# DeltaNet's decay and beta columns computed between tiles of the RG-LRU, on the PSUM tiles of its gates

## The chip, the cores and the metric

The kernel runs on one core of one Trainium2 chip. The metric is the device time of one launch in microseconds (us), as the median of several runs. In the text PE is TensorE (its matmuls), PEld its weight loads, DVE is VectorE, ACT ScalarE, POOL GpSimd and SP SyncE, which here only issues DMAs.

## The reference

One layer of a hybrid decoder on 576 tokens (512 of a prompt and 8 x 8 of samples), model width 1024, in float32. After a norm, one projection `w_in` feeds three branches: an RG-LRU, an S5 state space model and a gated DeltaNet. Their outputs are merged under sigmoid gates, projected and followed by a SwiGLU block. The parts that matter here:

```python
def rglru_branch(xr, gate_in, conv_buf, h0, conv_w, conv_b, wa, ba, wx, bx, lam, w_o):
    xc, new_buf = causal_conv(xr, conv_buf, conv_w)
    xc = xc + conv_b
    xb = xc.reshape(B, T, RG_BLOCKS, RG_BLOCK)
    r = jax.nn.sigmoid(jnp.einsum("btni,nij->btnj", xb, wa).reshape(B, T, RG_WIDTH) + ba)
    i = jax.nn.sigmoid(jnp.einsum("btni,nij->btnj", xb, wx).reshape(B, T, RG_WIDTH) + bx)
    log_a = -RG_C * r * jax.nn.softplus(-lam)
    inp = jnp.sqrt(-jnp.expm1(2.0 * log_a)) * (i * xc)
    h = linear_scan(jnp.exp(log_a), inp, h0)
    return (h * jax.nn.gelu(gate_in)) @ w_o, new_buf, h[:, -1]

# in gdn_branch
    beta = jax.nn.sigmoid(b_in)                                  # (tokens, 4 heads)
    g = -jnp.exp(a_log) * jax.nn.softplus(a_in + dt_bias)        # (tokens, 4 heads)
# in chunk_gated_delta, chunks of 64 tokens
    gc = jnp.cumsum(g, axis=-1)
    decay = jnp.where(causal, jnp.exp(gc[..., :, None] - gc[..., None, :]), 0.0)
```

`beta` and `gc` are the beta and decay columns: 8 numbers for each token, 4 heads of each.

## The kernel before, in words

Activations lie transposed, 128 channels on the partitions and 576 tokens in two halves of 288 columns. A float32 product is made of three fp32r matmuls: the weights are split into a high part `wh` (ACT, L181) and a low part `wl` (DVE, L182), the activations into `hh` and `hl` (for the merge `brh` and `brl`, L236 and L237), and L199, L200 and L201 multiply hh·wh, hl·wh and hh·wl. A raw weight tile `wr` comes by DMA (issued by SP); `wr` has 2 buffers, `wh` and `wl` have 4 each, of 4 k-tiles of 128 rows, so one split feeds 24 matmuls.

PSUM is divided by pools. The projections' and merge's sums `mm` have 3 slots. Tag "sm" has 3 slots: S5's `gtp`, `ktp`, `xp`, `s5yp`, and in the kernel before also `abc`, `gcps` and `bgp`. Tag "sr", which the helper `sr(name)` allocates, has 2 slots and holds the RG-LRU's gate sums `gps` (L748) in this part of the program.

The code is written in this order: S5 in four tiles (`s5_front` and `s5_chain`, L828 to L832); `rg(0)` to `rg(3)`, the RG-LRU's four tiles; five merge gates `g1`; the block of the beta and decay columns (L837 to L905); then the merge of the RG-LRU (`merge("rg_wo", ...)`, tiles 0 to 6, L910), and DeltaNet (`gdn_qkv`, `gdn_prep`). The instructions do not run in the order of the code: a scheduler places each engine's instructions by readiness, priority (the splits of weights stand first) and free slots of the pools, and each engine then runs its list strictly in order. An instruction that waits holds up everything behind it on its engine.

A tile of the RG-LRU, `rg(m)`: two projections, a convolution (L420, DVE), `xc`, four gate matmuls `gps` (L748) each read by a tanh `rgt` on ACT (L749), then exp, tanh and square root (L754 to L758, ACT), products and a scan on DVE (L756 to L769), and the product with the gelu gate (L773). `hout` takes the last states and leaves by `o["rg_h"]` (L907). `tsplit` (L236, L237) splits the result for the merge.

A chain of S5, `s5_chain(m)`: products `z`, the scan `zs` (L674, two for each tile, DVE), `st` (L686), the matmuls `s5yp` (L699, L700), the sum `s5y` (L702, DVE), a gelu (L722 to L726) and eight DMAs `ys` (L707).

The block of the columns: 32 narrow matmuls `abps` (L849), transposes `abc` (L854), a tanh for `beta`, a chain of small softplus instructions on DVE (L120 to L160, then L871, all on 128x20), the cumulative sums `gcps` (L873 to L878, PE), `gc` (L882), exponentials, a transpose `bgp` (L901), its copy `bgs` on ACT (L903), which takes a buffer of S5's scratch (`S5Z`), and a DMA of `bgs` to `bgd` in DRAM (L905). `gdn_prep` reads `bgd` back, spread over the partitions, as `bet` and `eg` (L969), and DVE subtracts `gc` (`dt`, L973).

Of the kernel before, what the change touches and what calls it, by code (L numbers as in the profile page):

```python
# [8 lines left out]
F32 = mybir.dt.float32  # L9
# [56 lines left out]
def hybrid_step(ctx: ExitStack, tc: tile.TileContext, i, o, dbg=None):  # L66
# [13 lines left out]
    def nm(s):  # L80
        cnt[0] += 1
        return f"{s}_{cnt[0]}"
# [9 lines left out]
    def P(k):  # L92
        a, w = PAR[k]
        return par[:, a:a + w]
# [132 lines left out]
    def each(ps, f):  # L227
        for a in range(2):
            f(ps[a], lambda t: t[:, NH * a:NH * a + NH])
# [13 lines left out]
    def tsplit(x, scale=None):  # L243
        return split(x, T("brh", F32R)[:, :NT], T("brl", F32R)[:, :NT], scale)
# [25 lines left out]
    def T(name, dt=F32):  # L270
        return tp.tile([128, TW], dt, name=nm(name), tag="T")

    def sr(name):
        return pss.tile([128, 512], F32, name=nm(name), tag="sr", bufs=2)
# [22 lines left out]
    pss = psx.enter_context(tc.tile_pool(name="pss", bufs=3, space=PSUM))  # L297
# [8 lines left out]
    def R(name):  # L306
        return rp.tile([128, NT], F32, name=nm(name), tag="R")
# [90 lines left out]
    def w_in(idx):  # L398
        return gemm(i["w_in"][idx], h)
# [4 lines left out]
    def pad_in(ps, hist, slot):  # L404
        pad = T("pad")
        smp = pad[:, SOFF:PADW].rearrange("p (b t) -> p b t", t=3 + NTS)
        S.activation(pad[:, 3:3 + NH], ps[0], AF.Copy)  # L407
        S.activation(pad[:, 3 + NH:SOFF], ps[1][:, 0:NP - NH], AF.Copy)
        S.activation(smp[:, :, 3:], ps[1][:, NP - NH:NH].rearrange("p (b t) -> p b t", t=NTS), AF.Copy)
        G.memset(pad[:, 0:3], 0.0)  # L410
        G.tensor_copy(smp[:, :, 0:3], hist.rearrange("p (b t) -> p b t", t=3))
        G.tensor_copy(cst[:, slot, 0, :], pad[:, NP:NP + 3])
        G.tensor_copy(cst[:, slot, 1:9, :], smp[:, :, NTS:])
        return pad

    def conv(pad, w, b):
        y = T("cv")
        S.activation(y[:, :CW], pad[:, 0:CW], AF.Identity, scale=w[0], bias=b)
        for k in range(1, 4):
            V.scalar_tensor_tensor(y[:, :CW], pad[:, k:k + CW], w[k], y[:, :CW], op0=OP.mult, op1=OP.add)  # L420
        return y

    def two_part(t):
        return t[:, 0:NP], t[:, SOFF:SOFF + 11 * NB].rearrange("p (b t) -> p b t", t=11)[:, :, 0:NTS]
# [296 lines left out]
    def gelu2(t, x, sq):  # L721
        S.activation(sq, x, AF.Square)  # L722
        S.activation(sq, sq, AF.Copy, scale=0.044715, bias=1.0)
        V.tensor_tensor(sq, sq, x, op=OP.mult)
        S.activation(sq, sq, AF.Tanh, scale=math.sqrt(2.0 / math.pi))
        V.scalar_tensor_tensor(t, sq, 1.0, x, op0=OP.add, op1=OP.mult)  # L726

    def rg(m):
        ps = w_in(IDX["rgx"] + m)
        pad = pad_in(ps, P("rg_hist")[:, 24 * m:24 * m + 24], m)  # L730
        ps = w_in(IDX["rgg"] + m)
        gx_ = T("rgx")
        each(ps, lambda p, c: S.activation(c(gx_), p, AF.Copy))
        w = P("rg_cw")[:, 4 * m:4 * m + 4]
        y = conv(pad, [w[:, a:a + 1] for a in range(4)], P("rg_cb")[:, m:m + 1])
        xc = R("xc")
        yp_, ys_ = two_part(y)
        S.activation(xc[:, 0:NP], yp_, AF.Copy)
        S.activation(xc[:, NP:NT].rearrange("p (b t) -> p b t", t=NTS), ys_, AF.Copy)
        gts = []  # L740
        rgw = cp.tile([128, 2, 128], F32, name=nm("rgw"), tag="rgw", bufs=2)
        DQ.dma_start(rgw, i["rg_w"][:, 2 * m:2 * m + 2, :])
        for a in range(2):
            t = R("rgt")
            for half in range(2):
                hs = slice(NH * half, NH * half + NH)
                gps = sr("gps")
                PE.matmul(gps[:, 0:NH], rgw[:, a, :], xc[:, hs], start=True, stop=True)  # L748
                S.activation(t[:, hs], gps[:, 0:NH], AF.Tanh, scale=0.5, bias=rc[:, 2 + a, m:m + 1])  # L749
            gts.append(t[:, :NT])  # L750
        tr, ti = gts
        a_ = y[:, :NT]
        th = tr
        S.activation(a_, tr, AF.Exp, scale=rc[:, 1, m:m + 1], bias=rc[:, 1, m:m + 1])  # L754
        S.activation(th, tr, AF.Tanh, scale=rc[:, 0, m:m + 1], bias=rc[:, 0, m:m + 1])
        V.scalar_tensor_tensor(a_, a_, 1.0, th, op0=OP.add, op1=OP.mult)  # L756
        S.activation(a_, a_, AF.Copy, scale=-1.0, bias=1.0)
        S.activation(th, th, AF.Sqrt)  # L758
        V.scalar_tensor_tensor(ti, ti, 1.0, xc[:, :NT], op0=OP.add, op1=OP.mult)
        V.scalar_tensor_tensor(th, a_, 1.0, th, op0=OP.add, op1=OP.mult)  # L760
        V.scalar_tensor_tensor(ti, ti, 0.5, th, op0=OP.mult, op1=OP.mult)
        t8 = cp.tile([128, 8], F32, name=nm("t8"), tag="t8")
        av = a_[:, NP:NT].rearrange("p (b t) -> p b t", t=NTS)[:, :, 0]
        bv = ti[:, NP:NT].rearrange("p (b t) -> p b t", t=NTS)[:, :, 0]
        V.tensor_tensor(t8, av, P("rg_h0")[:, 8 * m:8 * m + 8], op=OP.mult)
        V.tensor_tensor(bv, bv, t8, op=OP.add)
        V.memset(av, 0.0)
        hh = y
        V.tensor_tensor_scan(hh[:, :NT], a_, ti, 0.0, op0=OP.mult, op1=OP.add)  # L769
        G.tensor_copy(hout[:, m, 0:1], hh[:, NP - 1:NP])  # L770
        G.tensor_copy(hout[:, m, 1:9], hh[:, NP:NT].rearrange("p (b t) -> p b t", t=NTS)[:, :, NTS - 1])
        gelu2(gx_[:, :NT], gx_[:, :NT], pad[:, :NT])
        V.tensor_tensor(gx_[:, :NT], hh[:, :NT], gx_[:, :NT], op=OP.mult)  # L773
        return gx_
# [10 lines left out]
    def gate(b, m, alloc=T):  # L785
        ps = w_in(IDX["gate"] + 8 * b + m)
        t = alloc("gt")
        each(ps, lambda p, c: S.activation(c(t), p, AF.Tanh, scale=0.5))
        return t
# [40 lines left out]
            fr[m + 1] = s5_front(m + 1)  # L830
        s5_chain(m, *fr[m])
    DQ.dma_start(o["s5"], s5o)  # L832
    rg_h = [rg(m) for m in range(3)]
    rg_h.append(rg(3))
    g1 = [gate(0, m) for m in range(5)]

    wab = cp.tile([128, 8, 8], F32, name="wab")  # L837
    SY.dma_start(wab, i["w_ab"])
# [5 lines left out]
    for half in range(2):  # L844
# [3 lines left out]
            for a in range(2):  # L848
                PE.matmul(ps[:16], wab_s[:, k, :], h[k][a][:, sl], start=k == 0 and a == 0, stop=k == KT - 1 and a == 1)  # L849
        S.activation(abr[:16, sl], ps[:16], AF.Copy)  # L850
    cps = pss.tile([128, 512], F32, name="abc", tag="sm")
    for n in range(5):
        w = 128 if n < 4 else 64
        PE.transpose(cps[:w, 16 * n:16 * n + 16], abr[0:16, 128 * n:128 * n + w], ident[0:16, 0:16])  # L854
    abc = cp.tile([128, 5, 8], F32, name="abcs")
# [13 lines left out]
    nA = cp.tile([128, 4], F32, name="nA")  # L869
    exp_cols(cp, nA, P("a_log"), 4)  # L870
    V.scalar_tensor_tensor(gcl, gcl, -1.0, nA[:, None, :].to_broadcast([128, 5, 4]), op0=OP.mult, op1=OP.mult)  # L871
    cps = pss.tile([128, 512], F32, name="gcps", tag="sm")
    PE.matmul(cps[:, 0:16], tri, gcl[:, 0:4, :], start=True, stop=True)  # L873
    PE.matmul(cps[:64, 16:20], C("tris")[:64], gcl[:64, 4, :], start=True, stop=True)
    PE.matmul(cps[:, 32:48], ones, gcl[:, 0:4, :], start=True, stop=True)
# [21 lines left out]
    bg = cp.tile([128, 8, 5], F32, name="bg")  # L897
    V.tensor_copy(bg[:, 0:4, :], beta.rearrange("p n h -> p h n"))
    V.tensor_copy(bg[:, 4:8, :], gc.rearrange("p n h -> p h n"))
    bgp = pss.tile([128, 512], F32, name="bgp", tag="sm")  # L900
    PE.transpose(bgp[:40, 0:128], bg.rearrange("p v n -> p (v n)"), ident)  # L901
    bgs = S5Z("bgs").rearrange("p a c -> p (a c)")[:40, 0:128]
    S.activation(bgs, bgp[:40, 0:128], AF.Copy)  # L903
    bgd = dr.tile([40, 128], F32, name="bgd")
    DQ.dma_start(bgd, bgs)  # L905

    DQ.dma_start(o["rg_h"], hout)  # L907
    rg_y = [tsplit(t[:, :NT]) for t in rg_h]

# [765 lines left out]
```

## Time and profile before

| | before |
|---|---|
| median of 3 runs | 1097.19 us (1095.03 to 1099.34) |
| the profiled execution | 1097.05 us |
| its span, first to last instruction | 1095.1 us |
| outside the span | 1.95 us |
| PE busy | 1034.5 us, 94% |
| DVE busy | 795.3 us, 73% |
| ACT busy | 487.3 us, 44% |
| POOL busy | 231.0 us, 21% |
| mean granted TensorE clock | 0.974 of full speed |

All times in the rows below are counted from the start of the span, in one profiled execution. A matmul's duration includes its time in the pipeline, so PE's rate is read from the distance of two starts and not from a duration.

### The profile page before, as it was taken

The numbers are of one execution on the slowest core, as the hardware profiler recorded it, in microseconds if no ns is written. First come the engines' busy times: TensorE is split into PE (matmuls) and PEld (weight loads), VectorE is DVE, ScalarE is ACT, GpSimd is POOL, SyncE is SP. The second block draws the span as 40 slices with busy tenths as digits, with TensorE's granted clock in tenths as the row PEclk, the third lists the DMA queues.
The fourth block names the chain that finished last, engine by engine and source line by source line (L and its number), as shares of the span: only waits on it lengthen the run. The fifth ranks groups of instructions, "written<-read, shape, count | busy, mean of one in ns | idle before, by whom it ended". The sixth has DMA issues, their size and how long they took to land.

```text
span 1095.1 us, 20057 instructions
## 1 busy us (share of the span) xinstructions
PE 1034.5 (94%) x7658; PEld 988.9 (90%) x7658; DVE 795.3 (73%) x1853; ACT 487.3 (44%) x971; POOL 231.0 (21%) x301
## 2 busy tenths in 40 slices
PE   5999999967999999999999899899999999999994
PEld 4799989967989889998899899899999999999994
DVE  7899989876997678743636747875676776867756
ACT  4258943424443433222333444354653635536620
POOL 1024111104532234221001331210111201112114
PEclk8999999988999999999999999999999999999997
DMA  6333223422323133212112621124564646746602
GB/s 204 92 103 103 72 82 83 113 67 92 102 84 90 68 110 101 83 54 107 59 53 69 227 91 58 59 73 130 135 177 95 155 125 135 183 92 140 164 1 87
DMA packets 69521, 112.74 MB, mean 103 GB/s; under 512 B 27434, under 2 KB 35762, under 8 KB 69426
## 3 DMA queue, kind: packets, MB, share of 16 engines
q1 hardware_dynamic: 61650, 97.31, 27.7%
q0 software_dynamic: 7776, 14.16, 8.0%
q8 instruction: 60, 0.98, 0.4%
q14 instruction: 35, 0.29, 0.1%
HBM read 103.20 MB, written 8.24 MB: 102 GB/s over the span
## 4 chain that ended last, share of the span: by engine, by line
PE 78%; DVE 12%; DMA 4%; ACT 3%; issue 2%; POOL 0%; SPq 0%; DVEq 0%; ACTq 0%; POOLq 0%
PE mm L199 11%; PE mm L200 11%; PE mm L201 11%; PE mm L1439 10%; PE mm L1441 10%; PE mm L1440 10%; PE mm L381 2%; DVE wl L182 2%; PE up L1183 1%; PE s5yp L700 1%; DMA wr<-in_w_gate 1%; PE gps L748 1%; PE s5yp L699 1%; ACT wh L181 1%; PE rows L262 1%
## 5 line engine op out<-in xcount | busy, mean ns | idle before, releaser
L181 ACT ACTIVATE wh<-wr 128x512 fp32r<-128x512 f32 x250 | 154.7, 628 | 221.8 <-PE mm L200 119.4
L199 PE MATMUL mm<-hh,wh 128*128 128x288 f32 x768 | 232.8, 304 | 6.8 <-ACT pad L407 5.4
L182 DVE TENSOR_TENSOR wl<-wr,wh 128x512 fp32r<-128x512 f32 x250 | 182.2, 736 | 77.9 <-ACT wh L181 75.5
L200 PE MATMUL mm<-hl,wh 128*128 128x288 f32 x768 | 231.2, 301 | 0.0
L201 PE MATMUL mm<-hh,wl 128*128 128x288 f32 x768 | 230.1, 300 | 0.0
L199 PEld LDWEIGHTS mm<-hh,wh 128*128 128x128 f32 x768 | 145.9, 190 | 12.7 <-ACT pad L407 5.7
L201 PEld LDWEIGHTS mm<-hh,wl 128*128 128x128 f32 x768 | 145.9, 190 | 2.8 <-issue 2.2
L200 PEld LDWEIGHTS mm<-hl,wh 128*128 128x128 f32 x768 | 146.0, 190 | 2.5 <-issue 1.7
L1441 PE MATMUL mm<-fh,wl 128*128 128x288 f32 x352 | 103.7, 295 | 0.0
L1439 PE MATMUL mm<-fh,wh 128*128 128x288 f32 x320 | 94.6, 296 | 0.0
L1440 PE MATMUL mm<-fl,wh 128*128 128x288 f32 x320 | 94.4, 295 | 0.0
L1441 PE MATMUL mm<-hfh,wl 128*128 128x288 f32 x288 | 84.5, 296 | 0.7 <-DMA wl<-in_w_gate 0.7
L1440 PE MATMUL mm<-hfl,wh 128*128 128x288 f32 x288 | 84.9, 295 | 0.0
L1439 PE MATMUL mm<-hfh,wh 128*128 128x288 f32 x288 | 84.8, 295 | 0.0
L199 PE MATMUL mm<-brh,wh 128*128 128x288 f32 x224 | 67.4, 305 | 4.3 <-DVE mg L802 1.8
L200 PE MATMUL mm<-brl,wh 128*128 128x288 f32 x224 | 68.1, 305 | 0.9 <-DVE brl L237 0.6
L201 PE MATMUL mm<-brh,wl 128*128 128x288 f32 x224 | 66.9, 299 | 0.0
L1441 PEld LDWEIGHTS mm<-fh,wl 128*128 128x128 f32 x352 | 66.1, 188 | 0.0
L1440 PE MATMUL mm<-t,wh 128*128 128x288 f32 x216 | 64.0, 297 | 0.0
L1441 PE MATMUL mm<-t,wl 128*128 128x288 f32 x216 | 63.7, 295 | 0.0
L1439 PE MATMUL mm<-t,wh 128*128 128x288 f32 x216 | 63.6, 295 | 0.0
L1439 PEld LDWEIGHTS mm<-fh,wh 128*128 128x128 f32 x320 | 60.0, 188 | 0.1
(501 smaller groups left out, 2575.9 us busy)
## 6 DMA issues: line engine op xcount, KB each, us to landing
wr<-in_w_in SPq DMA_DIRECT2D x48, 512.0 KB, 3.5
wr<-in_w_gate SPq DMA_DIRECT2D x22, 512.0 KB, 3.9
wr<-in_w_up SPq DMA_DIRECT2D x22, 512.0 KB, 4.2
wr<-in_w_down SPq DMA_DIRECT2D x20, 512.0 KB, 4.9
wl<-in_w_gate POOLq DMA_DIRECT2D x27, 256.0 KB, 4.5
wl<-in_w_up POOLq DMA_DIRECT2D x27, 256.0 KB, 4.3
wr<-in_w_out SPq DMA_DIRECT2D x8, 512.0 KB, 3.5
xa<-in_x SPq DMA_DIRECT2D x8, 288.0 KB, 6.3
```

The source lines that it names most:

```text
L181: S.activation(hi, raw, AF.Copy)
L182: (eng or lo_eng()).tensor_tensor(lo, raw, hi.bitcast(F32), op=OP.subtract)
L199: PE.matmul(acc, hi[:, k, :], xh[:, sl], start=k0 + k == 0, stop=False)
L200: PE.matmul(acc, hi[:, k, :], xl[:, sl], start=False, stop=False)
L201: PE.matmul(acc, lo[:, k, :], xh[:, sl], start=False, stop=k0 + k == n - 1)
L262: m0 = PE.matmul(rows[:, 96 * b:96 * b + 96], rc[:96, b:b + 1].to_broadcast([96, 128]), ident[:96, :96], start=True, stop=True).ins
L381: PE.matmul(ps, uw[m][k], xa[:, k, hsl(half)], start=k == 0, stop=k == KT - 1)
L699: PE.matmul(ypv[:, b_, :], tm[:, g, :], x[:, g, :], start=True, stop=False)
L700: PE.matmul(ypv[:, b_, :], cl[g // 4][:, g % 4, 1:9, :].rearrange("p d h -> p (d h)"), st[:, g, :], start=False, stop=True)
L1439: PE.matmul(acc, hi[:, k0 + k, :], xh, start=new and k == 0, stop=False, skip_group_check=not new)
L1440: PE.matmul(acc, hi[:, k0 + k, :], xl, start=False, stop=False, skip_group_check=not new)
L1441: PE.matmul(acc, lo[:, k0 + k, :], xh, start=False, stop=k == len(x) - 1, skip_group_check=not new)
```

## The change

`rg(2)`, `rg(3)` and the five gates move behind the block of the columns, so the block stands between `rg(1)` and `rg(2)` in the code. Its three PSUM tiles `abc`, `gcps` and `bgp` are taken from tag "sr" (2 slots, the gate sums' tag) in place of "sm" (3 slots, S5's).

```diff
-    rg_h = [rg(m) for m in range(3)]
-    rg_h.append(rg(3))
-    g1 = [gate(0, m) for m in range(5)]
+    rg_h = [rg(m) for m in range(2)]
...
-    cps = pss.tile([128, 512], F32, name="abc", tag="sm")
+    cps = sr("abc")
...
-    cps = pss.tile([128, 512], F32, name="gcps", tag="sm")
+    cps = sr("gcps")
...
-    bgp = pss.tile([128, 512], F32, name="bgp", tag="sm")
+    bgp = sr("bgp")
...
     DQ.dma_start(bgd, bgs)
 
+    rg_h += [rg(m) for m in range(2, 4)]
+    g1 = [gate(0, m) for m in range(5)]
     DQ.dma_start(o["rg_h"], hout)
```

The scheduler turns this into a different list on each engine. The first place is PE at the end of S5, in the kernel before. The names are those of the words above; `sqp` holds column sums of DeltaNet's q.

```order
L700 MATMUL s5yp_1333<-st_1299,cl_1161 128x72
L699 MATMUL s5yp_1333<-s5x_1108,tm_1117 128x72
L700 MATMUL s5yp_1333<-st_1299,cl_1161 128x72
L873 MATMUL gcps<-gcl,con 128x16
L874 MATMUL gcps<-gcl,con 64x4
L875 MATMUL gcps<-gcl,con 128x16
L876 MATMUL gcps<-gcl,con 64x4
L878 MATMUL gcps<-con,gcl 128x8 x4
L901 MATMUL bgp<-con,bg 40x128
L931 MATMUL sqp_3005<-sq_3003,con 32x288 x2
L199 MATMUL mm_3098<-hh_123,wh_3089 128x288
```

The same place in the changed kernel:

```order
L700 MATMUL s5yp_1333<-st_1299,cl_1161 128x72
L699 MATMUL s5yp_1333<-s5x_1108,tm_1117 128x72
L700 MATMUL s5yp_1333<-st_1299,cl_1161 128x72
L199 MATMUL mm_2730<-hh_123,wh_2721 128x288
L200 MATMUL mm_2730<-hl_124,wh_2721 128x288
L201 MATMUL mm_2730<-hh_123,wl_2722 128x288
```

`gcps` and `bgp` no longer stand behind S5's last matmul. In the kernel before 144 matmuls of L199 to L201 lie between the last `s5yp` and `sqp_3245`, and in the changed kernel 384; from `sqp_3245` on the two lists run nearly alike.

The second place is PE where the changed kernel's `bgp` now stands, ahead of S5's second half. `mm_2554`, `mm_2555` and `mm_2589` are sums of the RG-LRU's merge, and `brh_2532`/`brl_2533` and so on the split results of `rg(0)` to `rg(3)`; 2532 is that of `rg(0)`, 2536 of `rg(1)`, 2540 of `rg(2)` and 2544 of `rg(3)`.

```order
L199 MATMUL mm_2554<-brh_2532,wh_2550 128x288
L199 MATMUL mm_2555<-brh_2532,wh_2550 128x288
L899 MATMUL bgp_1858<-con,bg 40x128
L748 MATMUL gps_2006<-xc_2000,rgw_2003 128x288
L199 MATMUL mm_2589<-brh_2532,wh_2585 128x288
L748 MATMUL gps_2009<-xc_2000,rgw_2003 128x288
L200 MATMUL mm_2554<-brl_2533,wh_2550 128x288
```

The four gate sums of `rg(2)` and the four of `rg(3)` follow from here on, among S5's matmuls. In the kernel before they stood far ahead, among the projections:

```order
L201 MATMUL mm_2073<-hh_127,wl_2065 128x288
L199 MATMUL mm_2073<-hh_129,wh_2064 128x288
L748 MATMUL gps_1852<-xc_1846,rgw_1849 128x288
L748 MATMUL gps_1855<-xc_1846,rgw_1849 128x288
L200 MATMUL mm_2073<-hl_130,wh_2064 128x288
L201 MATMUL mm_2073<-hh_129,wl_2065 128x288
```

What moved: all eight gate sums of `rg(2)` and `rg(3)`, from a place among the projections to one behind `bgp`. The three merge sums that surround them fill all three `mm` slots.

The third place is DVE, where the last split result of the RG-LRU, `brl_2545`, is made. In the kernel before it stands right behind S5's first scan, `zs_870`:

```order
L674 SCALAR_TENSOR_TENSOR zs_870<-rho_871,z_859 128x256 x2
L693 TENSOR_TENSOR s5y_898<-s5x_661,par 128x576
L237 TENSOR_TENSOR brl_2541<-rgx_1838,brh_2540 128x576
L182 TENSOR_TENSOR wl_2654<-wr_2651,wh_2653 128x512
L616 TENSOR_TENSOR bl_959<-bl_959,tb_960 128x512
L237 TENSOR_TENSOR brl_2545<-rgx_2014,brh_2544 128x576
```

In the changed kernel it stands two of S5's tiles later, ahead of the third scan, `zs_1218`:

```order
L769 SCALAR_TENSOR_TENSOR cv_2171<-cv_2171,rgt_2188 128x576
L726 SCALAR_TENSOR_TENSOR s5y_1072<-s5sq_1094,s5y_1072 128x576
L620 TENSOR_TENSOR cl_1161<-cl_1161,tb_1162 128x576
L773 TENSOR_TENSOR rgx_2168<-cv_2171,rgx_2168 128x576
L237 TENSOR_TENSOR brl_2545<-rgx_2168,brh_2544 128x576
L662 TENSOR_TENSOR z_1207<-zt_249_1208,zt_250_1209 128x256
L667 TENSOR_TENSOR z_1207<-zt_251_1213,zt_252_1214 128x256
L674 SCALAR_TENSOR_TENSOR zs_1218<-rho_1219,z_1207 128x256 x2
```

What moved: the tails of `rg(2)` and `rg(3)` (L756 to L773 and L237) on DVE, from ahead of S5's first scan and just behind it to places among S5's chains. The small softplus instructions moved the other way, from S5's last tile to places ahead of its first scan.

## Rows read from the trace of the kernel before

**Rows 1.** The page's part 1: busy us (share of the span) and instructions

```profile
PE 1034.5 (94%) x7658; PEld 988.9 (90%) x7658; DVE 795.3 (73%) x1853; ACT 487.3 (44%) x971; POOL 231.0 (21%) x301
```

**Rows 2.** Waits of PE, 20 to 300 us: instruction, releaser, total us, times, longest

```profile
PE gcps L873 <- DVE gcl L871: 7.1, 1, 7.1
PE mm L199 <- ACT pad L407: 5.4, 1, 5.4
...
PE sqp L931 <- ACT sq L952: 1.5, 1, 1.5
PE bgp L901 <- DVE bg L899: 0.6, 1, 0.6
```

**Rows 3.** The chain that ended last, 223 to 262 us: start, us, engine, tile, line

```profile
233.34 0.24 PE s5yp L700 x2
...
240.66 0.58 PE gcps L873 x2
...
245.53 1.33 DMA bgd<-bgs
...
247.41 5.05 DMA eg<-bgd
```

**Rows 4.** Windows: us, busy of PE, PEld, DVE, ACT, POOL, then granted clock, DMA

```profile
156.70:208.00 51.30, 48.86 (x386) 46.70 (x385) 46.66 (x103) 18.62 (x39) 8.17 (x13) 0.97 0.37 98
...
233.40:275.40 42.00, 27.34 (x169) 25.46 (x170) 26.97 (x70) 17.25 (x40) 11.35 (x21) 0.76 0.27 84
156.70:233.60 76.90, 74.42 (x588) 71.81 (x587) 69.15 (x165) 28.23 (x59) 14.12 (x30) 0.98 0.34 88
```

**Rows 5.** Timeline of PE, end of the stretch: start, us, line, output<-inputs

```profile
274.01 0.29 PE L199 MATMUL mm<-hh,wh 128*128 128x288 f32 x1
...
274.80 0.29 PE L199 MATMUL mm<-hh,wh 128*128 128x288 f32 x1
...
275.29 0.44 PE L931 MATMUL sqp<-sq,con 128*32 128x288 f32 x2
```

**Rows 6.** Timeline of PE after a wait; in brackets the idle time and its releaser

```profile
164.18 0.40 PE L199 MATMUL mm<-brh,wh 128*128 128x288 f32 x1 [1.85 <-DVE mg L802]
...
167.72 0.38 PE L199 MATMUL mm<-brh,wh 128*128 128x288 f32 x1
```

**Rows 7.** Timeline of DVE up to S5's first scan

```profile
146.35 0.68 DVE L182 TENSOR_TENSOR wl<-wr,wh 128x512 fp32r<-128x512 f32 x1
...
156.75 0.68 DVE L674 TENSOR_TENSOR_SCAN zs<-rho,z 128x256 f32<-128x256 f32 x1
```

**Rows 8.** The tile brl: durations ns min, median, max; first and last start

```profile
L237 DVE TENSOR_TENSOR brl<-rgx,brh x4: 744/759/760, 153.3 to 160.5; 128x576 fp32r<-128x576 f32 x4
```

**Rows 9.** Groups of DVE, 60 to 160 us: count | busy us, mean ns

```profile
L182 DVE TENSOR_TENSOR wl<-wr,wh 128x512 fp32r<-128x512 f32 x25 | 17.0, 680 | 3.9 <-ACT wh L181 3.9
...
L769 DVE TENSOR_TENSOR_SCAN cv<-cv,rgt 128x576 f32<-128x576 f32 x4 | 5.4, 1346 | 0.0
```

**Rows 10.** Waits of DVE, 120 to 262 us, as in Rows 2

```profile
DVE dt L973 <- DMA eg<-bgd: 6.6, 1, 6.6
...
DVE mg L802 <- PE mm L201: 1.9, 1, 1.9
```

**Rows 11.** The tile gps: durations ns min, median, max; first and last start

```profile
L748 PE MATMUL gps<-xc,rgw x32: 403/406/510, 74.4 to 130.1; 128*128 128x288 f32 x32
L749 ACT ACTIVATE rgt<-gps,rgc x16: 487/500/519, 75.1 to 131.5; 128x288 f32<-128x288 f32 x16
```

**Rows 12.** Timeline of ACT around a load of its function table

```profile
132.38 0.68 ACT L757 ACTIVATE cv<-cv 128x576 f32<-128x576 f32 x1
133.08 1.28 ACT L758 ACT_TABLE_LOAD   x1
134.37 0.69 ACT L758 ACTIVATE rgt<-rgt 128x576 f32<-128x576 f32 x1
```

## The prediction

> **What bounds the kernel now.** I began with the page's part 1 [rows 1]: PE is busy for 1034.5 of 1095.1 us, so a change is worth what it does to PE's idle time and to its clock. Second came PE's waits [rows 2]. Around the stretch that the change touches four of them lie between 240 and 265 us: 7.1 for `gcps`, 0.6 for `bgp`, 1.5 for `sqp` and 5.4 for an `mm`. The reader is to see that the first two wait for DVE's softplus and for `gc`, and that the last has an ACT evacuation as its releaser although the cause lies further back. The chain of waits shows it [rows 3]: S5's last `s5yp` ends near 233.5, the softplus runs on DVE until PE gets `gcps` at 240.66, `bgd` is written at 245.53, `eg` is issued at 247.41 and takes 5.05 to land, and DVE sits idle 6.6 us for it [rows 10], with the splits and convolutions that PE needs queued behind. Third, the windows [rows 4]: from 233.4 to 275.4 PE is busy 27.34 of 42.0 us, at a granted clock of 0.76. Ahead of that, from 156.7 to 208, PE is busy for 48.86 of 51.3 us: there it lacks nothing. S5's chains on DVE (69.15 busy of 76.9 us) are covered by large matmuls. That cover is what the change touches.
>
> **What the change removes.** At full clock two L199 matmuls three apart start at 274.01 and 274.80 [rows 5], 0.132 us for one. Between S5's last `s5yp` and `sqp_3245` (275.29) stand 144 of them and the small sums, which is 19.0 us of work in 41.9 us. The idle time there is 7.1 + 0.6 + 1.5 + 5.4 = 14.6 us. What remains, 41.9 - 19.0 - 14.6 = 8.3 us, is about 1.6 for the small sums (which I put at 12 starts of `gcps` and two of `bgp` and `sqp` near 0.12) and 6.7 of slow clock. If `gcps` has been done long before, the 7.1 and 0.6 vanish; the 1.5 and 5.4 vanish because `eg` is no longer what DVE waits for while PE is out of work; and PE, never idle, keeps its clock. Taken alone that is up to 14.6 + 6.7 = 21.3 us, and 1075.8 us.
>
> **What it costs.** The order shows that the 21 us are not free. The work that PE has left at S5's end is 384 large matmuls to `sqp_3245`, not 144: 240 more, 240 x 0.132 = 31.7 us. They were cover under S5's chains and now come after. The cause is the move of `rg(2)` and `rg(3)`. In the kernel before the four `brl` lie between 153.3 and 160.5 [rows 8], so the merge's matmuls run from 164 on. In the changed kernel `brl_2545` stands on DVE ahead of S5's third scan. Adding up DVE's rows of that order with the durations of the same lines here puts 45.6 us of DVE work between the first scan and it. Until then `mm_2554`, `mm_2555` and `mm_2589` hold all three `mm` slots with sums that cannot be finished, and PE has only S5's small matmuls and the `gps`. So PE will starve for most of 156 to 203, and I expect some 30 us of idle time there.
>
> The end of the stretch is then the end T of S5's last `s5yp`, plus 384 x 0.132 = 50.7, plus 0.6 for `sqp_3005`: T + 51.3, against 275.3 now. At T the clock will be low; the one short stall here whose end the rows show, 1.85 us, was followed by 16 matmuls at (167.72 - 164.18) / 15 = 0.24 us [rows 6], which is 16 x (0.24 - 0.132) = 1.7 us more than at full clock. I take 1.7 once; the bounds are 0, if S5's last tile with its large matmuls has raised the clock before T, and 6.7, what the slow clock cost in the stretch of rows 4.
>
> T follows from DVE. **First scan.** Ahead of it DVE has 28 splits `wl` in the changed order, 29 before. Before, the 28th starts at 146.35 [rows 7]; it waits for PE to free a weight slot, so DVE's smaller work (two tails of the RG-LRU less) cannot bring it much forward. Behind it stand 5.5 us of DVE work up to the scan: 146.35 + 0.7 + 5.5 = 152.5. PE has the 32 `abps` ahead of it in addition (32 x 0.132 = 4.2 us) and eight `gps` less (8 x 0.41 = 3.3 us [rows 11]), so +0.9: 153.4, against 156.75 now. **From there to the end.** DVE's work between the first scan and the last `s5y` is the same in both orders within 1 us: 9 splits at 0.68, 4 `mg`, 2 convolution steps and some twenty softplus instructions go out, and two tails at about 6 us each (one scan at 1.35 [rows 9], five products at 0.75, a `brl` at 0.76 and small ones) come in: 67.0 and 67.7 us by the sum of the rows. Before, the way from 156.75 to 233.4 took 76.65, so about 9 us were waits or gaps. If DVE waits as before, except for the 1.9 us that it stood for the merge's matmul [rows 10], T = 153.4 + 76.65 - 1.9 = 228.2. If it never waits, T = 153.4 + 67.7 = 221.1.
>
> Sum: 228.2 + 51.3 + 1.7 - 275.3 = **+5.9 us**. From `sqp_3245` on the orders of PE agree nearly, and DVE, which has 35 us of work (27 of rows 4 and the 8 us of splits and `mg` that were done before S5's end) in the 51 us, is there in time; I carry the shift to the end with 1.5 us either way. Against the profiled execution's own 1097.05: **1103 us**. The median of the runs, 1097.19, is 0.14 above that execution.
>
> **Edits costed at nothing.** The softplus on DVE ahead of the first scan (about 26 instructions of 0.1 to 0.2 us, some 4 us of work) is hidden in the wait for weight slots; without that cover the first scan moves by up to 4 us. `abc`, `gcps` and `bgp` on "sr" relieve S5's three slots, but hold the gates' two: `gcps` goes through one, `bgp` stays in it until ACT has made `bgs`, and `bgs` takes a buffer of S5's scratch, so it comes near S5's end. All eight `gps` thus go through one slot. SP: `bgd` still stands behind `out_s` and the third tile's `ys`, and `bet` and `eg` behind the last tile's eight `ys`. So `eg` lands 13 to 19 us after T (19.1 now), not early. That is hidden this time, because PE has 31.7 us more work behind T that needs nothing of `eg`; without the cover it costs the 5.4 of rows 2. `out_rg_h` now waits on SP for the last RG-LRU tile, with weight loads behind it, in the stretch in which no weights are wanted, since the slots are full.
>
> On ACT's side, two pairs of function table loads now stand among S5's chains. The rows show a load from 133.08 to 134.36, the activation behind it at 134.37, and the one ahead of it ending at 133.06 [rows 12], so a switch costs 1.28 us. The Trainium skill, "ScalarE: Activation LUTs", section "What ACT_TABLE_LOAD costs", has the same load and a drain of some 1.38 us on top, 2.66 together; by that the four loads would add an estimated 5.5 us to ACT in the chain and the sum could come out near 1108. The trace shows no drain, and ACT is busy for less than half of that window, so the rows decide.
>
> **The rivals.**
> (a) DVE does not wait: T = 221.1, no loss of clock: 221.1 + 51.3 - 275.3 = -2.9, or **1094 us**. For it: the changed order has fewer splits among the chains, and these were part of the waits. Against it: PE's results for S5 come at a lower clock, and the tails of the RG-LRU bring ACT hops of their own. The price even on this side is bounded, and that is why I think a clear gain unlikely: no sum of DVE's rows lets S5 end early enough. To win more than 5.5 us T would have to be below 218.5.
> (b) The single gate slot bites, and the kernel is clearly slower: each `gps` waits until the `rgt` of the one before has been read, and PE, in order, holds S5's matmuls behind it. A hop is 0.41 + 0.50 us [rows 11], eight make 7.3 us, so T = 235.5 and the time is **1110 us**. It decides from the point where DVE has run out of other work when a `gps` is blocked. The Trainium skill, "Perfetto Trace Analysis", section "Identifying Performance Opportunities", says that a gap that repeats on the engine that should be full can mean too few PSUM buffers for the next tile; it speaks against giving gate slots and `mm` slots away, and no row of before shows such a repeated gap.
> (c) The change doesn't do what it says: `gcps` is early, but `eg` is not, and DVE's wait stays. If `eg` keeps its 19 us behind S5's end, DVE idles up to 6.6 us [rows 10] ahead of splits that PE needs from about T + 24 on. Mostly hidden; at worst 5.9 + 6.6, **1109.5 us**.
> (d) The whole cover is regained: PE never starves, because the `mm` slots come free otherwise, and the 21.3 us are won: **1076 us**. The order excludes it as far as I can see; it needs `brl_2545` 40 us earlier than DVE's list allows.
>
> **How the numbers follow.** The forecast, 1100 to 1106, has 0.45; (a) 0.2; (b) 0.25, with the remainder of T's spread above; (c) 0.07; (d) or a first scan so early that (a) ends below 1091.7, 0.03. A measurement of this kernel tells about 0.5% from no change, 5.5 us, so "same" is 1091.7 to 1102.7, and the forecast's own range lies across the upper bound: half of it, with (a) but for its lowest part, is "same": 0.22 + 0.18 = 0.40. "Faster" is (d) and the low end of (a), 0.07. "Slower" is the rest, 0.53. The range reaches from (a) less 1.5 for what follows, 1093, to (b) plus 1.5, 1112.
>
> **What would show it.** Right: PE's wait for `gcps` and its 5.4 us for `pad` are gone; new waits of PE, together about 30 us, stand between 156 and 205, released by DVE (`brl`, `st`, `mg`); the last `s5yp` ends at 225 to 232; the clock is low within that stretch and full from T + 4 to 280; `sqp_3245` runs at 279 to 284. Wrong: if PE's idle time between 156 and 205 is under 15 us, the starving was overrated, and if T lies above 238, the gate slot or ACT decided.

## The result, and the profile after

The changed kernel takes 1106.52 us (median of 5 runs, 1103.4 to 1109.79), the kernel before 1096.44 in the same comparison: a ratio of 1.008, with a 95% interval of 1.006 to 1.010. It is slower, as forecast, by 10 us in place of 6. The median lies just above the forecast's own 1100 to 1106 and inside the whole range of 1093 to 1112. The profiled execution of the changed kernel took 1108.24 us with a span of 1106.4, against 1097.05 and 1095.1.

First the page's part 1 and the granted clock of part 2 (40 slices of the span, in tenths of full speed), which answer to [rows 1]:

```profile
span 1106.4 us, 20060 instructions
PE 1047.5 (95%) x7658; PEld 999.0 (90%) x7658; DVE 797.5 (72%) x1853; ACT 487.6 (44%) x971; POOL 231.3 (21%) x301
...
PEclk9999995699999999999999999999999999999997
```

PE is busy for longer with the same 7658 instructions, and the clock has a hole in the seventh and eighth slice, 166 to 221 us. A busy PE at a low clock is not more work. Next, PE's waits from 20 to 300 us, as in [rows 2]:

```profile
PE ktp L632 <- DVE cl L620: 3.9, 2, 2.1
PE mm L199 <- DVE mg L802: 3.7, 3, 3.2
...
PE ktp L632 <- DVE rgt L766: 3.2, 1, 3.2
PE s5yp L700 <- DVE st L686: 1.3, 1, 1.3
```

The waits for `gcps`, `bgp`, `sqp` and `pad` are gone. New ones have come, and they stand not after S5 but within it, released by DVE's work for S5 (`cl`, `st`), for the RG-LRU (`rgt`) and for the merge (`mg`, which empties a `mm` slot). The windows below are, like [rows 4], first the stretch under S5's chains, then 5 us within it, then the stretch from S5's last `s5yp` to `sqp_3245`:

```profile
156.70:208.00 51.30, 38.01 (x196) 32.40 (x197) 46.32 (x103) 29.04 (x53) 8.00 (x18) 0.60 0.25 54
...
190.00:195.00 5.00, 1.74 (x12) 0.95 (x12) 5.00 (x9) 2.52 (x4) 0.70 (x1) 0.50 0.01 3
...
230.60:282.40 51.80, 51.80 (x391) 51.01 (x392) 32.26 (x56) 26.26 (x54) 11.91 (x28) 1.00 0.38 120
```

In the first one PE issues 196 matmuls where it issued 386 before, with 13.3 us idle (2.4 before) and a clock of 0.60 (0.97 before). The 190 matmuls that are missing, at 0.132 us, are 25 us of work. In the last one PE is never idle and at full clock: it does what it could not do before. The places behind these numbers are, from the view of the tile `brl` (durations in ns, first and last start), the split results:

```profile
L237 DVE TENSOR_TENSOR brl<-rgx,brh x4: 743/751/758, 155.6 to 197.0; 128x576 fp32r<-128x576 f32 x4
```

from the view of line 674, S5's scans:

```profile
L674 DVE TENSOR_TENSOR_SCAN zs<-rho,z x8: 661/672/692, 148.7 to 217.4; 128x256 f32<-128x256 f32 x8
```

and from the timeline of PE the end of the stretch:

```profile
282.35 0.68 PE L931 MATMUL sqp<-sq,con 128*32 128x288 f32 x4
```

The last `brl` starts at 197.0 in place of 160.5 [rows 8], the first scan at 148.7 in place of 156.75 [rows 7], and `sqp_3245` at 282.35 in place of 275.29 [rows 5]. That is +7.1 us in the stretch. The transposed norms after DeltaNet (L1204) come 8.8 us later and the end of the span 11.3 us later.

### The profile page after: what moved, and what is told of

The parts are those of the page before. It is cut to its first block, busy times and chain, and to the rows that moved or that the text cites. A ratio compares the mean times of both kernels' runs of the same rounds, so it can differ in the third digit from the quotient of the medians.

```text
span 1106.4 us, 20060 instructions
## 1 busy us (share of the span) xinstructions
PE 1047.5 (95%) x7658; PEld 999.0 (90%) x7658; DVE 797.5 (72%) x1853; ACT 487.6 (44%) x971; POOL 231.3 (21%) x301
## 4 chain that ended last, share of the span: by engine, by line
PE 77%; DVE 12%; DMA 5%; ACT 3%; issue 2%; SPq 0%; POOL 0%; DVEq 0%; ACTq 0%; POOLq 0%
PE mm L199 12%; PE mm L201 12%; PE mm L200 12%; PE mm L1441 9%; PE mm L1439 9%; PE mm L1440 9%; PE mm L381 2%; DVE wl L182 2%; DMA wr<-in_w_gate 1%; DMA xa<-in_x 1%; DMA wl<-in_w_gate 1%; PE up L1183 1%; PE xp L648 1%; PE zq L1165 1%; DVE x L1304 1%
## 5 line engine op out<-in xcount | busy, mean ns | idle before, releaser
L199 PE MATMUL mm<-hh,wh 128*128 128x288 f32 x768 | 232.6, 304 | 0.7 <-ACT glt L819 0.5
L200 PE MATMUL mm<-hl,wh 128*128 128x288 f32 x768 | 230.5, 300 | 0.0
L201 PE MATMUL mm<-hh,wl 128*128 128x288 f32 x768 | 230.1, 300 | 0.0
L199 PEld LDWEIGHTS mm<-hh,wh 128*128 128x128 f32 x768 | 145.8, 190 | 7.3 <-issue 4.0
L201 PEld LDWEIGHTS mm<-hh,wl 128*128 128x128 f32 x768 | 145.8, 190 | 2.3 <-issue 1.9
L1439 PE MATMUL mm<-fh,wh 128*128 128x288 f32 x320 | 94.7, 296 | 0.1
L199 PE MATMUL mm<-brh,wh 128*128 128x288 f32 x224 | 68.2, 310 | 9.5 <-ACT glt L819 3.5
L201 PE MATMUL mm<-brh,wl 128*128 128x288 f32 x224 | 68.6, 307 | 0.0
L1410 POOL DMA_DIRECT2D wl<-in_w_up x27 | 23.3, 863 | 178.0 <-ACT wl L1409 73.1
```

Source lines behind the costliest of these rows:

```text
L199: PE.matmul(acc, hi[:, k, :], xh[:, sl], start=k0 + k == 0, stop=False)
L200: PE.matmul(acc, hi[:, k, :], xl[:, sl], start=False, stop=False)
L201: PE.matmul(acc, lo[:, k, :], xh[:, sl], start=False, stop=k0 + k == n - 1)
L1410: G.dma_start(lo, src, accum_op=OP.add)
L1439: PE.matmul(acc, hi[:, k0 + k, :], xh, start=new and k == 0, stop=False, skip_group_check=not new)
```

## The experiments

Two questions were asked. Is it the late tails of `rg(2)` and `rg(3)` that cost, or the gate slot that the columns hold, or the moved code as such? And what of the stall in the kernel before could have been won?

**The tag alone.** The code in the order of before, the three tiles from "sr":

```diff
-    cps = pss.tile([128, 512], F32, name="abc", tag="sm")
+    cps = sr("abc")
...
-    cps = pss.tile([128, 512], F32, name="gcps", tag="sm")
+    cps = sr("gcps")
...
-    bgp = pss.tile([128, 512], F32, name="bgp", tag="sm")
+    bgp = sr("bgp")
```

> The kernel before in its own order of the code, with the three tiles abc, gcps and bgp on the gates' tag sr instead of S5's tag sm, and nothing else. On PE's list the gate sums of all four RG-LRU tiles keep their places among the projections, gcps and bgp come ahead of S5's last tile, and 144 large matmuls stand behind S5's last s5yp, as in the kernel before. Theory (the loss is the starving by the late tails of rg(2) and rg(3), the gain is the lost wait for gcps): no starving here, so no loss. PE's 7.1 and 0.6 us for gcps and bgp go, and bgd leaves before S5's end, but bet and eg stay behind the last ys on SP, so DVE still waits for eg, which lands some 5.4 us earlier: about 1091 us, 1088 to 1094. Rival 1 (the tag is what costs: one slot for gates and columns): 1100 us or more. Rival 2 (all idle time between 240 and 260 goes): 1076 us.

Measured: 1094.18 us, ratio 0.9981 (0.9959 to 1.0003). Not told from no change, and just above the 1088 to 1094 of the theory; the profiled execution is one of the short ones (span 1089.0). Its waits of PE from 20 to 300 us, and from the timeline of PE its `sqp_3245`:

```profile
PE mm L199 <- ACT pad L407: 6.3, 1, 6.3
PE sqp L931 <- ACT sq L952: 5.7, 1, 5.7
```

```profile
271.01 0.68 PE L931 MATMUL sqp<-sq,con 128*32 128x288 f32 x4
```

The 7.1 and 0.6 us for `gcps` and `bgp` are gone, without starving, and what followed them has grown: `sqp` from 1.5 to 5.7, `pad` from 5.4 to 6.3. Of the 7.7 us taken away, 4.3 arrive at `sqp_3245`. So the tag frees the columns to go early and costs nothing that can be told here; rival 1 falls, and so does rival 2, for the next wait was late by itself.

**The move alone.** The changed kernel with the tiles back on "sm":

```diff
-    cps = sr("abc")
+    cps = pss.tile([128, 512], F32, name="abc", tag="sm")
...
-    cps = sr("gcps")
+    cps = pss.tile([128, 512], F32, name="gcps", tag="sm")
...
-    bgp = sr("bgp")
+    bgp = pss.tile([128, 512], F32, name="bgp", tag="sm")
```

> The changed kernel with abc, gcps and bgp back on S5's tag sm, so that only the code is moved: the block stands between rg(1) and rg(2), the tiles are those of before. PE's list then has abc near S5's end, gcps and bgp behind the last s5yp, all gate sums among the projections and 144 large matmuls behind S5, as before. Theory (the place of the instructions decides, and the tag is what frees the block to go early): 1096 us as before, 1093 to 1099, with the wait for gcps of about 7 us in place. Rival (to write rg(2) and rg(3) behind the block costs by itself): 1102 us or more.

Measured: 1101.32 us, ratio 1.0050 (1.0032 to 1.0067). The wait for `gcps` is back, as expected, but the kernel is slower than before, which was the rival's side (1102 or more); the theory's 1093 to 1099 is missed. PE's waits from 20 to 300 us, then the tile `brl`, then line 700 with the last `s5yp` (first and last start):

```profile
PE gcps L871 <- DVE gcl L869: 6.7, 1, 6.7
```

```profile
L237 DVE TENSOR_TENSOR brl<-rgx,brh x4: 746/750/760, 157.4 to 164.6; 128x576 fp32r<-128x576 f32 x4
```

```profile
L700 PE MATMUL s5yp<-st,cl x64: 223/275/302, 164.2 to 236.5; 128*128 128x72 f32 x64
```

All gate sums stand early here, yet the last `brl` starts 4 us later than before and S5 ends 3.2 us later (236.5 against 233.3). The move alone thus costs 5.4 us (1095.91 for the kernel before in that comparison), some 3 of them through S5's chains on DVE, which have the end of the RG-LRU's tails among them. Between the first scan and S5's end DVE is idle 10.7 us (7.8 before); its largest waits there are 2.9 for `mg`, 2.6 for a `wl` and 2.2 for `s5y` (before 1.9, 0.2 and none). These are small waits in several places, and no run separates them.

**All four tiles ahead of the block, tag "sr".** The block stands between `rg(3)` and the gates:

```diff
     rg_h.append(rg(3))
-    g1 = [gate(0, m) for m in range(5)]
...
     DQ.dma_start(bgd, bgs)
 
+    g1 = [gate(0, m) for m in range(5)]
     DQ.dma_start(o["rg_h"], hout)
```

The three tiles are taken from "sr" as above.

> The block on the tag sr, written behind rg(3) and ahead of the five gates: all four RG-LRU tiles stand ahead of it. On PE's list abc, gcps and bgp come well inside S5 (gcps some 320 places ahead of the last s5yp), the gate sums stay among the projections, 144 large matmuls behind S5. Theory: as with the tag alone, about 1091 us, 1087 to 1094; bgd leaves earlier, but eg is read back behind the last ys all the same, so little is won over the tag alone. Rival (the tag costs, or an early block takes DVE from S5's chains): 1097 us or more.

Measured: 1097.84 us, ratio 1.0016 (0.9998 to 1.0034). No gain, and no loss that can be told from no change. The theory's 1087 to 1094 is missed, and the median lies in the rival's range (1097 or more). The last `brl` starts at 166.5, PE starves little (79.48 busy of 83.6 us from the first scan to S5's end), but S5 ends at 242 instead of 233.5, and DVE still waits 8.6 us for `eg`. Columns that are made early are no gain in themselves here.

**One tail late.** The block between `rg(2)` and `rg(3)`:

```diff
-    rg_h = [rg(m) for m in range(2)]
+    rg_h = [rg(m) for m in range(3)]
...
-    rg_h += [rg(m) for m in range(2, 4)]
+    rg_h += [rg(m) for m in range(3, 4)]
```

> The changed kernel with the block one tile later, between rg(2) and rg(3): only the four gate sums of rg(3) come behind bgp, and 275 large matmuls stand behind S5's last s5yp (before 144, changed 384). Theory (time is T, the end of S5, plus 0.132 us for each of these, and T grows with the number of tails that stand among S5's chains): T about 231, 231 + 36.3 + 0.6 + 1.7 = 269.6, or 1092 us, 1089 to 1098. Rival (any gate sum behind bgp starves PE as much as eight do, since the three mm slots wait for the last brl in either case): 1103 us or more.

Measured: 1101.22 us, ratio 1.0053 (1.0033 to 1.0073). Half of the changed kernel's loss; the theory's 1089 to 1098 and the rival's 1103 are both missed. The last `brl` starts at 183.1 and S5 ends at 233.4. By the working of the expectation `sqp_3245` would have come at 270, but it comes at 277.6, since PE still waits 3.1 us at `pad` and 0.9 at `sqp` and has a clock of 0.8 to 0.86 from 255 to 275: with 275 matmuls behind S5 the wait for `eg` is covered only in part.

**Three tails late.** The block behind `rg(0)`:

```diff
-    rg_h = [rg(m) for m in range(2)]
+    rg_h = [rg(0)]
...
-    rg_h += [rg(m) for m in range(2, 4)]
+    rg_h += [rg(m) for m in range(1, 4)]
```

> The changed kernel with the block one tile earlier, behind rg(0): three tails of the RG-LRU (twelve gate sums) stand behind bgp, and 444 large matmuls behind S5's last s5yp (before 144, split behind rg(2) 275, changed kernel 384). Theory (late tails starve PE, and what it leaves undone comes behind S5): S5 ends near 230 as in the changed kernel, 230 + 444 x 0.132 + 1 = 289.6 for sqp_3245, 1113 us, 1109 to 1118. Rival (the loss comes from the gate slot that bgp holds, the same for two or three tails): 1106 us.

Measured: 1111.86 us, ratio 1.0152 (1.0122 to 1.0182), as the theory had it. `sqp_3245` comes at 289.56 (289.6 expected), the last `brl` at 212.8, S5 ends at 228.1. That the place is met to 0.1 us is in part luck: S5 ends 2 us earlier than the expectation put it, and the way behind is 2 us longer. Its PE waits from 140 to 292 us also show what rival (b) of the prediction described, which the changed kernel does not have:

```profile
PE s5yp L700 <- DVE st L686: 8.7, 3, 8.1
PE gps L748 <- ACT rgt L749: 7.8, 4, 5.2
```

With twelve gate sums through the slots PE waits 7.8 us for the `rgt` ahead. In the changed kernel with eight there is no such row of 0.3 us or more.

**The slot freed early.** The changed kernel, with `bgs` in a tile that is free:

```diff
-    bgs = S5Z("bgs").rearrange("p a c -> p (a c)")[:40, 0:128]
+    bgs = abr[:40, 0:128]
```

> The changed kernel, with bgs written into abr, which is free by then, in place of a buffer of S5's scratch. ACT can copy bgp early, its slot comes free, and the gate sums of rg(2) and rg(3) have two slots in place of one; their places behind bgp and the late tails on DVE stay. 336 large matmuls stand behind S5's last s5yp (384 in the changed kernel). Theory (the backlog behind S5 is the price, 0.132 us for each matmul): the changed kernel's S5 end of 230.5 kept, sqp_3245 comes 48 x 0.132 = 6.3 us earlier, 1100 us, 1097 to 1104. Rival (the single gate slot was the price): S5 ends some 7 us earlier as well, 1094 us or less. Second rival (neither: the clock in the starved stretch): 1106 us.

Measured: 1103.23 us, ratio 1.0062 (1.0036 to 1.0088). With a second gate slot the last `gps` starts at 171.2 (178.8 in the changed kernel), but S5 ends only 1.6 us earlier (228.8 against 230.4), not 7, so the single slot was not the price. But `sqp_3245` stays at 282.23: 48 matmuls fewer stand behind S5, and a wait of 5.7 us at `sqp` has come back. So the time lies in the theory's range of 1097 to 1104, but not by its mechanism, which wanted `sqp_3245` 6.3 us earlier. The backlog of the changed kernel was also cover.

**The other half of the stall.** DVE's subtractions `dt`, which wait for `eg`, are queued behind the convolution of the first head's v, once on the tag alone and once on the kernel before:

```diff
-            V.scalar_tensor_tensor(dst[:, NP:NT].rearrange("p (b t) -> p b t", t=NTS), ts_, 1.0, ys_,
-                                   op0=OP.add, op1=OP.mult)
+            vi = V.scalar_tensor_tensor(dst[:, NP:NT].rearrange("p (b t) -> p b t", t=NTS), ts_, 1.0, ys_,
+                                        op0=OP.add, op1=OP.mult).ins
...
-        st_.update(kqe=kqe, v2=dst)
+        st_.update(kqe=kqe, v2=dst, vi=vi)
...
+        with tc.issue_after(hs_[0]["vi"]) if hd < 2 else nullcontext():
             for n in range(4):
                 V.tensor_scalar(dt[:, n, :], eg[:, 128 * n:128 * n + 128], gc[:, n, hd:hd + 1], 0.0,
                                 op0=OP.subtract, op1=OP.min)
```

> The kernel with the tag sr alone (order of the code as before), in which DVE's subtractions dt (L973, five for each of the first two heads) are queued on DVE behind the convolution of the first head's v; nothing else. With the tag alone DVE waited 8.7 us for eg with the convolutions of k and v queued behind, and PE waited 5.7 us at sqp and 6.3 us at pad. Theory (what is left of the stall is DVE's in-order wait for eg): the 6.3 us of pad go and the clock stays up, 1087 us, 1083 to 1091. Rival (PE is then held by something else of the same length, the convolutions or ACT's pad): 1094 us, as with the tag alone.

> The kernel before with the same queueing of dt behind the convolution of the first head's v, and nothing else: tags and order of the code as before. PE's 7.1 us for gcps stays, the 5.4 us at pad should go. Theory: 1091 us, 1088 to 1094, and the two together (with the tag) win more than either. Rival (the stall as a whole hangs on the late columns, so nothing is won while gcps stands behind S5): 1096 us.

Measured: with the tag 1089.74 us, ratio 0.9946 (0.9930 to 0.9962), faster than both kernels and in the theory's range; on the kernel before 1094.96, ratio 0.9989 (0.9970 to 1.0007), no change that can be told, with the theory's 1088 to 1094 missed and the rival's 1096 not excluded. PE's waits from 140 to 292 us with the tag, and its `sqp_3245`:

```profile
PE sqp L931 <- ACT sq L952: 8.4, 2, 5.7
```

```profile
266.98 0.68 PE L931 MATMUL sqp<-sq,con 128*32 128x288 f32 x4 [2.69 <-ACT sq L952]
```

The 6.3 us at `pad` are gone, and DVE no longer waits for `eg`. `sqp_3245` comes at 266.98, 8.3 us earlier than before and 4.0 earlier than with the tag alone, although S5 ends 2.7 us later than before (236.0 against 233.3). On the kernel before the 5.4 us at `pad` go too, but 7.1 for `gcps` stay. Its `sqp_3245` comes at 268.27, 7.0 us earlier than before, and yet its span is only 2.2 us shorter: with `dt` later, `sqp_3245` no longer tells what the kernel wins. Only the two together are clear of noise, so the late columns were one part of the stall; whether together they win more than the sum of the two alone, the intervals don't tell.

## Why the prediction was right, point by point

The sign, the place and the mechanism held. The size of the change was under-estimated (5.9 us forecast, 10 measured). In the stretch itself the shift was 7.1 us, and that this is so near the sum is in part luck: S5's end came 2.3 us later than forecast, the way behind it took 0.5 us more, and the 1.7 us for the clock were not paid.

*What goes.* Confirmed: none of the four waits of [rows 2] is left, and PE is at full clock and without a gap from S5's end to `sqp_3245`. The columns are early, `gcps` is done at 149. DVE waits for `eg` only 1.8 us, behind 240 large matmuls of cover, as the part on the edits costed at nothing said.

*The backlog.* Confirmed. From the last `s5yp` at 230.5 to `sqp_3245` at 282.35 lie 51.85 us; the working had T + 51.3. The 1.7 us for a low clock at T were not paid: the clock is 1.00 from 215 on, and the large matmuls had run again without a gap from 206 to 211.6, as the prediction's lower bound had it. The window ahead of S5's end:

```profile
225.00:230.00 5.00, 5.00 (x44) 5.00 (x42) 2.48 (x7) 0.50 (x2) 0.00 (x0) 1.00 0.53 128
```

The working holds only while the backlog covers the wait for `eg`: with three tails late it meets `sqp_3245`, with one tail late and with the slot freed early it puts it 7 to 8 us too early, since waits of PE stand again behind S5 there.

*The starving.* Right in cause and place, wrong in kind. `brl_2545` comes at 197.0, where the sum of DVE's rows had 199; but it started from a scan that came 4.7 us earlier than the sum had it, so the way from there took 48.3 us and not 45.6. I expected some 30 us of idle time between 156 and 205; 12.5 were idle there (2.4 before). That is under the 15 us which the prediction itself named as the sign that the starving was overrated, and as idle time it was. The sum held all the same, because it counts the matmuls left and not the idle time. The rest of what PE lost went at a low clock: in the five-us windows from 170 to 210 the granted clock is 0.50, the lower of the two levels, and PE is busy 0.19 us for each matmul from 156.7 to 208, where it was 0.13 before; how much of this is the clock alone no run separates. One who looks for idle time alone sees less than half of it.

*T.* 228.2 forecast, 230.5 measured, through two errors that nearly cancel. The first scan came at 148.7 and not at 153.4. The step that failed is that DVE's smaller work "cannot bring it much forward", said of the 28th split: it starts 3.8 us earlier, at 142.56 in place of 146.35, and the +0.9 us for PE's work does not show (timeline of DVE).

```profile
142.56 0.69 DVE L182 TENSOR_TENSOR wl<-wr,wh 128x512 fp32r<-128x512 f32 x1 [0.90 <-ACT wh L181]
```

The way from this split to the scan is the 6.2 us of the sum. And from there to S5's end it took 81.8 us and not 74.75. DVE's work is as the sum had it (69.31 busy, 67.7 by the sum), but DVE waits more, above all for PE's `s5yp` (waits of DVE, 120 to 262 us, as in [rows 10]; a larger one, 10.2 us for `wh`, has 7.8 of them behind S5's end):

```profile
DVE s5y L702 <- PE s5yp L700: 6.9, 4, 2.6
DVE dt L973 <- DMA eg<-bgd: 1.8, 2, 1.3
```

`s5y` waits 6.9 us for PE's `s5yp` (0.2 before), 5.8 of them ahead of S5's last `s5yp`. The places are in the timelines of DVE and of PE:

```profile
229.16 0.45 DVE L702 TENSOR_TENSOR s5y<-s5y,s5yp 128x288 f32<-128x288 f32 x1 [2.07 <-PE s5yp L700]
```

```profile
227.44 0.33 PE L700 MATMUL s5yp<-st,cl 128*128 128x72 f32 x2
```

PE is not slow there by its clock, which is 1.00 in S5's last tile. `s5yp` stands on PE's list behind large matmuls that PE is catching up on: DVE's last `st` is done at 225.56, the `s5yp` start at 227.44, and the large matmuls ahead of them run without a gap from 224.2. In the third tile it is the same, with `st` done at 207.26, 23 large matmuls from 206.05 on and `s5yp` at 211.61; there the clock adds to it, for 21 of them start 0.24 us apart and not 0.132. In the kernel before, the last tile's first such `s5yp` start at 230.25, ahead of the last `st`. I took "as before, less 1.9" for the waits; that is the mis-sized term inside T.

*What follows.* This is the term that missed most: 1.5 us either way forecast, 4.2 measured in the profiled executions (11.3 at the end against 7.1 at `sqp_3245`). A part has a row: PE waits 3.5 us in S5's output gate (timelines of PE and of ACT),

```profile
315.44 0.40 PE L199 MATMUL mm<-brh,wh 128*128 128x288 f32 x1 [3.49 <-ACT glt L819]
```

```profile
314.31 0.68 ACT L239 ACTIVATE brh<-yg 128x576 fp32r<-128x576 f32 x1 [5.00 <-DVE ssk L1004]
```

where it waited 0.4 before (4.0 against 1.4 with a second wait for `glt`), and ACT's split there waited for DVE. DVE, which in [rows 4] had done splits and `mg` before S5's end, does these after it now; that this is why it is late here is argued, not shown. I had said that it would be in time. At L1204 the shift is 8.8 us. The other 2.5 us come after 590 us, where the lists of the two kernels run alike; the five executions' spans lie between 1101.6 and 1107.9, and no experiment separates this part from their spread. Nor do the traces show the 4.2 us as a cost of late tails: from `sqp_3245` to the end of the span it is 819.8 us before and 824.1 after the change, but 820.1 with three tails late, and 817.3 to 824.6 over all the profiled executions here. The cause of this part stays open.

*The rivals.* (a) fell: DVE waited, though the first scan came earlier than even (a) had it. (b) has the measured time near its number, 1110, but not its mechanism: `gps` does not wait in the changed kernel, and a second slot brought S5's end 1.6 us forward in place of 7.3. (c) does not show: `eg` is covered. (d) fell, as the order said. What no rival held is that the move alone, without any gate sum behind the columns and with the old stall in place, is slower than before by 0.5%. So not all of the loss needs late gate sums.

| | matmuls behind S5's end | last `brl` starts | S5's last `s5yp` | `sqp_3245` | ratio to before |
|---|---|---|---|---|---|
| before | 144 | 160.5 | 233.3 | 275.29 | |
| tag alone | 144 | 159.8 | 234.6 | 271.01 | 0.998 |
| move alone | 144 | 164.6 | 236.5 | 278.27 | 1.005 |
| four tiles ahead, tag | 144 | 166.5 | 241.8 | 279.16 | 1.002 |
| one tail late | 275 | 183.1 | 233.2 | 277.59 | 1.005 |
| changed | 384 | 197.0 | 230.4 | 282.35 | 1.008 |
| three tails late | 444 | 212.8 | 227.9 | 289.56 | 1.015 |

From "four tiles ahead" down the rows differ by the place of the block alone, one RG-LRU tile for each row, with the tag the same (the gates `g1` stand behind the block in all four): the ratio goes from 1.002 over 1.005 and 1.008 to 1.015 as the last `brl` comes later. That is what shows the late tails as the cause. The table also shows the exchange: in the three rows with late tails each tail more brings S5's end 2.5 to 3 us forward, which fits DVE's having fewer splits `wl` to do before it (40, 35 and 33 start ahead of it; 45 before the change), and adds 60 to 109 matmuls behind it, 8 to 14 us.

## What to carry to other kernels

Before a chain is moved ahead to remove a stall, look at what stands there now as cover: PE was 95% busy under S5's chains (48.86 of 51.3 us) because the merge's matmuls were ready, and what made them ready was the work that was moved away. Compare what is left to do at the end of the stretch, not the stall, and count idle time and a low clock together. If a stall consists of two waits in a row, each one alone may win nothing: freeing the columns' PSUM slot and moving DVE's wait for `eg` behind ready work won 0.5% together here, and neither alone could be told from no change.

## What the runs showed that was not expected

An engine that is starved by another delays that other in turn when it catches up: the large matmuls that PE could not do in time stand ahead of S5's matmuls on its list, and DVE waited 6.9 us for these where it had waited 0.2, 4.3 of them at full clock. And PE's share of busy time did not fall with the loss: it went from 94.5 to 94.7% (1034.5 of 1095.1 us, 1047.5 of 1106.4), with the same number of instructions and a longer span.
